# Top-2 dispatch on one core: groups of 64 and 64 rows, eight equal stores, no early store, logits in one transfer

## The chip, the cores and the metric

The kernel runs on one core of a Trainium2 chip. The metric is the device time of one execution in microseconds; lower is better. Before the change the median of three runs is 239.2 us (239.19 to 239.37).

## The reference

For each of 16,384 tokens there are 512 values in `x` and 8 router logits. The two largest softmax probabilities of a token, divided by their sum, become two weights, and the output holds the token's 512 values twice: once times the smaller weight, once times the larger.

```python
probs = np.exp(router_logits - logits_max)
probs = probs / np.sum(probs, axis=-1, keepdims=True)
topk_indices = np.argsort(probs, axis=-1)[..., -k:]          # k = 2
topk_probs = np.take_along_axis(probs, topk_indices, axis=-1)
topk_probs = topk_probs / np.sum(topk_probs, axis=-1, keepdims=True)
x_expanded = x[:, :, np.newaxis, :].repeat(k, axis=2)
return x_expanded * topk_probs[..., np.newaxis]
```

The softmax's denominator cancels, so the two weights are the sigmoid of minus and of plus the difference between the largest and the second largest logit. Read are 33.55 MB of x and 0.52 MB of logits, written are 67.11 MB.

## The kernel before, in words

A *row* below is one token of each of the 128 partitions: 128 x 512 floats, 0.262 MB in x and 0.524 MB in the output, since each value is written twice. There are 128 rows. They are worked off in two groups, `GROUPS = [65, 63]`. Within a group, partition p owns G consecutive tokens (G is 65 or 63), so that one partition's part of a transfer of n rows is one contiguous run of n x 2 KB in x and n x 4 KB in the output. The distance in memory from one partition's run to the next is G x 2 KB in x and G x 4 KB in the output.

Three tiles lie in the core's on-chip memory. `xs` has 65 slots of one x row. `osp` has 18 slots of one output row. `WA` holds the two weights of all 128 rows. The logits are loaded into the last slot of `osp`, and the scratch of the top-2 search lies in the two slots before it.

The work goes in this order, written out by hand in two tables:

- `LOADS` gives the x loads of each group, by their number of rows: 6, 28, 31 for the first group, 32 and 31 for the second. All are issued on the SP queue (line 112). After the first of them come the two logits transfers (lines 105 and 106), and then `top2_weights` (lines 53 to 68): eleven VectorE instructions, which keep the larger and the smaller of pairs of logits, and two sigmoids on ScalarE.
- `STORES` gives for each store the number of rows, the place where the output rows are built (`osp` or `xs`, and the first slot), the number of its rows that ScalarE builds (`by_act`), and the queue. The other rows are built by one VectorE multiplication (line 127). A ScalarE row takes two activations (line 135). Line 138 issues the store.

A store whose home is `xs` is built in place: 16 input rows that sit in the upper half of a region of 32 slots are spread over the whole region as 16 output rows. The stores of a group alternate: one of 16 rows into `osp`, then one in place, then again one into `osp`, which must wait until the earlier store from `osp` has landed, and one of 15 rows in place. The first group has a small store of 2 rows ahead of these, which alone goes through the ACT queue.

Every other transfer is issued by SP, in program order, and SP waits in front of each issue until the data is built or the slots are free. The loads of the second group stand behind the fourth large store of the first group in this order. The second of them writes slots that this store reads, so SP waits until it has landed.

Of the kernel before, what the change touches and what calls it, by code (L numbers as in the profile page):

```python
# [1 line left out]

# [4 lines left out]

F32 = mybir.dt.float32
ALU = mybir.AluOpType
ACTF = mybir.ActivationFunctionType  # L10
P = 128
E = 8
D = 512


GROUPS = [65, 63]
M = sum(GROUPS)


LOADS = [[6, 28, 31], [32, 31]]  # L20


STORES = [
    [
        (2, ("osp", 0), 0, "ACT"),
        (16, ("osp", 2), 0, "SP"),
        (16, ("x", 2), 0, "SP"),
        (16, ("osp", 0), 4, "SP"),
        (15, ("x", 35), 0, "SP"),
    ],  # L30
    [
        (16, ("osp", 0), 1, "SP"),
        (16, ("x", 0), 0, "SP"),
        (16, ("osp", 0), 4, "SP"),
        (15, ("x", 33), 0, "SP"),
    ],
]
OSP = 18


def top2_weights(nc, scratch, logits, WA):

    used = [0]

    def cut(n):
        a = scratch[:, used[0] : used[0] + M * n].rearrange("p (m n) -> p m n", n=n)
        used[0] += M * n
        return a

    a, b = logits[:, :, 0:4], logits[:, :, 4:8]  # L50
    hi = cut(4)
    lo = b
    nc.vector.tensor_tensor(hi, a, b, op=ALU.max)  # L53
    nc.vector.tensor_tensor(lo, a, b, op=ALU.min)  # L54
    n = 4
    while n > 1:
        n //= 2
        a, b = hi[:, :, 0:n], hi[:, :, n : 2 * n]
        nhi, nlo, tmp = cut(n), cut(n), cut(n)
        nc.vector.tensor_tensor(tmp, lo[:, :, 0:n], lo[:, :, n : 2 * n], op=ALU.max)  # L60
        nc.vector.tensor_tensor(nlo, a, b, op=ALU.min)  # L61
        nc.vector.tensor_tensor(nlo, nlo, tmp, op=ALU.max)  # L62
        nc.vector.tensor_tensor(nhi, a, b, op=ALU.max)  # L63
        hi, lo = nhi, nlo
    dlt = cut(1)
    nc.vector.tensor_tensor(dlt, hi, lo, op=ALU.subtract)  # L66
    nc.scalar.activation(WA[:, :, 0], dlt[:, :, 0], ACTF.Sigmoid, scale=-1.0)  # L67
    nc.scalar.activation(WA[:, :, 1], dlt[:, :, 0], ACTF.Sigmoid, scale=1.0)  # L68


@with_exitstack
def kernel(
    ctx: ExitStack,
    tc: tile.TileContext,
    x: bass.AP,
    router_logits: bass.AP,
    k: bass.AP,
    out: bass.AP,
):
    nc = tc.nc  # L80
    N = x.shape[0] * x.shape[1]
    assert int(k) == 2 and router_logits.shape[-1] == E and x.shape[2] == D
    assert N == P * M
    xf = x.rearrange("b s d -> (b s) d")
    of = out.rearrange("b s k d -> (b s) k d")
    rf = router_logits.rearrange("b s e -> (b s) e")
    x_v, o_v, rl_v = [], [], []
    t0 = 0
    for n in GROUPS:
        t1 = t0 + P * n  # L90
        x_v.append(xf[t0:t1].rearrange("(p m) d -> p m d", p=P))
        o_v.append(of[t0:t1].rearrange("(p m) k d -> p m k d", p=P))
        rl_v.append(rf[t0:t1].rearrange("(p m) e -> p m e", p=P))
        t0 = t1

    pool = ctx.enter_context(tc.tile_pool(name="pool", bufs=1))
    xs = pool.tile([P, max(GROUPS), D], F32)
    osp = pool.tile([P, OSP, 2, D], F32)
    WA = pool.tile([P, M, 2], F32)

    logits = osp[:, OSP - 1].rearrange("p k d -> p (k d)").rearrange("p (m e) -> p m e", e=E)
    scratch = osp[:, OSP - 3 : OSP - 1].rearrange("p r k d -> p (r k d)")

    def load_logits():
        nc.sync.dma_start(logits[:, : GROUPS[0]], rl_v[0])  # L105
        nc.sync.dma_start(logits[:, GROUPS[0] :], rl_v[1])  # L106

    m0 = 0
    for g, G in enumerate(GROUPS):
        r = 0  # L110
        for n in LOADS[g]:
            nc.sync.dma_start(xs[:, r : r + n, :], x_v[g][:, r : r + n, :])  # L112
            if g == 0 and r < 6 <= r + n:
                load_logits()
                top2_weights(nc, scratch, logits, WA)
            r += n
        assert r == G
        r = 0
        for n, (home, a), by_act, queue in STORES[g]:
            if home == "x":  # L120
                og = xs[:, a : a + 2 * n, :].rearrange("p (r k) d -> p r k d", k=2)
            else:
                og = osp[:, a : a + n]
            v = n - by_act
            w = WA[:, m0 + r : m0 + r + n, :]
            if v:
                nc.vector.tensor_tensor(  # L127
                    og[:, :v],
                    xs[:, r : r + v, :].unsqueeze(2).to_broadcast([P, v, 2, D]),
                    w[:, :v].unsqueeze(3).to_broadcast([P, v, 2, D]),  # L130
                    op=ALU.mult,
                )
            for i in range(v, n):
                for c in range(2):
                    nc.scalar.activation(  # L135
                        og[:, i, c], xs[:, r + i, :], ACTF.Copy, scale=w[:, i, c : c + 1]
                    )
            {"SP": nc.sync, "ACT": nc.scalar}[queue].dma_start(o_v[g][:, r : r + n], og)  # L138
            r += n
        assert r == G  # L140
        m0 += G


# [1 line left out]
_INS = ['x', 'router_logits', 'k']  # L145
_OUTS = [((16, 1024, 2, 512), 'float32')]

_NUMBERS = {'k': 2}


# [26 lines left out]
```

## Time and profile before

| What | Value |
|---|---|
| median of three runs | 239.2 us |
| the profiled execution, its own time | 239.38 us |
| its span, first to last instruction | 237.6 us |
| VectorE busy | 132.2 us, 20 instructions |
| ScalarE busy | 13.2 us, 21 instructions |
| moved by DMA | 101.19 MB |
| mean rate over the span | 426 GB/s |
| share of the 16 DMA engines' span taken by packets | 97.7% on SP's queue, 1.0% on ACT's |

In the profile DVE is VectorE, ACT is ScalarE, SP is the engine that issues nearly all transfers; SPq and ACTq are their issue queues. q1 is the queue that SP feeds and q10 the one that ACT feeds. Times in a row count from the start of the span. A DMA issue row gives the time from the issue to the moment when the whole transfer has landed.

### The profile page before, as it was taken

The numbers are of one execution on the slowest core, as the hardware profiler recorded it, in microseconds if no ns is written. First come the engines' busy times: TensorE is split into PE (matmuls) and PEld (weight loads), VectorE is DVE, ScalarE is ACT, GpSimd is POOL, SyncE is SP. The second block draws the span as 40 slices with busy tenths as digits, with TensorE's granted clock in tenths as the row PEclk, the third lists the DMA queues.
The fourth block names the chain that finished last, engine by engine and source line by source line (L and its number), as shares of the span: only waits on it lengthen the run. The fifth ranks groups of instructions, "written<-read, shape, count | busy, mean of one in ns | idle before, by whom it ended". The sixth has DMA issues, their size and how long they took to land.

```text
span 237.6 us, 124 instructions
## 1 busy us (share of the span) xinstructions
DVE 132.2 (56%) x20; ACT 13.2 (6%) x21; POOL 0.2 (0%) x4
## 2 busy tenths in 40 slices
DVE  0640599999289999000000009999956999920000
ACT  2000000000080000000000001000006100000000
POOL 0000000000000000000000000000000000000000
DMA  7979989898989989899998989898989989897995
GB/s 265 541 338 488 408 386 535 348 530 353 496 386 441 441 353 530 353 508 414 414 519 353 508 370 502 353 519 353 496 386 419 463 353 530 353 530 342 496 445 217
DMA packets 2304, 101.19 MB, mean 426 GB/s; under 512 B 256, under 2 KB 384, under 8 KB 512
## 3 DMA queue, kind: packets, MB, share of 16 engines
q1 hardware_dynamic: 2160, 100.14, 97.7%
q10 hardware_dynamic: 144, 1.05, 1.0%
HBM read 34.08 MB, written 67.11 MB: 426 GB/s over the span
## 4 chain that ended last, share of the span: by engine, by line
DMA 48%; DVE 39%; SPq 1%; issue 0%; DVEq 0%
DMA xs<-in_x_dram 30%; DVE osp L127 25%; DMA out_dram<-osp 19%; DVE xs L127 14%; SPq L105 0%; SPq L106 0%; SPq L112 0%; SPq L138 0%; DVEq L127 0%
## 5 line engine op out<-in xcount | busy, mean ns | idle before, releaser
L127 DVE TENSOR_TENSOR osp<-xs,WA 128x12288 f32<-128x12288 f32 (+3 forms) x5 | 61.6, 12318 | 68.7 <-DMA xs<-in_x_dram 58.4
L127 DVE TENSOR_TENSOR xs<-xs,WA 128x16384 f32<-128x16384 f32 (+1 forms) x4 | 66.8, 16692 | 0.3
L135 ACT ACTIVATE osp<-xs,WA 128x512 f32<-128x512 f32 x18 | 11.4, 709 | 161.3 <-DMA out_dram<-osp 90.0
L53 DVE TENSOR_TENSOR osp<-osp 128x512 f32<-128x512 f32 x1 | 0.7, 692 | 8.2 <-DMA osp<-in_router_logits_dram 8.2
L67 ACT ACT_TABLE_LOAD x1 | 1.3, 1283 | 0.7 <-PEq L158 0.7
L67 ACT ACTIVATE WA<-osp 128x128 f32<-128x128 f32 x1 | 0.3, 316 | 10.1 <-DVE osp L66 10.1
L54 DVE TENSOR_TENSOR osp<-osp 128x512 f32<-128x512 f32 x1 | 0.7, 693 | 0.0
L60 DVE TENSOR_TENSOR osp<-osp 128x256 f32<-128x256 f32 (+1 forms) x2 | 0.7, 352 | 0.0
L62 DVE TENSOR_TENSOR osp<-osp 128x256 f32<-128x256 f32 (+1 forms) x2 | 0.7, 352 | 0.0
L63 DVE TENSOR_TENSOR osp<-osp 128x256 f32<-128x256 f32 (+1 forms) x2 | 0.7, 352 | 0.0
L61 DVE TENSOR_TENSOR osp<-osp 128x256 f32<-128x256 f32 (+1 forms) x2 | 0.7, 351 | 0.0
L66 DVE TENSOR_TENSOR osp<-osp 128x128 f32<-128x128 f32 x1 | 0.3, 292 | 0.0
L68 ACT ACTIVATE WA<-osp 128x128 f32<-128x128 f32 x1 | 0.3, 298 | 0.0
L158 POOL MEMSET const-bfloat16-1.0<- 128x1 bf16 x1 | 0.1, 102 | 0.0
L158 POOL MEMSET const-uint8-127<- 128x1 uint8 x1 | 0.1, 102 | 0.0
L158 POOL MEMSET const-float32-0.0<- 128x1 f32 x1 | 0.1, 99 | 0.2 <-issue 0.2
L158 POOL MEMSET const-float32-1.0<- 128x1 f32 x1 | 0.1, 99 | 0.0
## 6 DMA issues: line engine op xcount, KB each, us to landing
xs<-in_x_dram SPq DMA_DIRECT2D x2, 7936.0 KB, 40.8
out_dram<-xs SPq DMA_DIRECT2D x2, 7680.0 KB, 27.5
xs<-in_x_dram SPq DMA_DIRECT2D x1, 7168.0 KB, 24.2
xs<-in_x_dram SPq DMA_DIRECT2D x1, 1536.0 KB, 6.0
out_dram<-osp ACTq DMA_DIRECT2D x1, 1024.0 KB, 24.5
osp<-in_router_logits_dram SPq DMA_DIRECT2D x1, 260.0 KB, 6.2
osp<-in_router_logits_dram SPq DMA_DIRECT2D x1, 252.0 KB, 6.4
out_dram<-osp SPq DMA_DIRECT2D x4, 23.9
```

Of the source, the lines that this page charges most:

```text
L53: nc.vector.tensor_tensor(hi, a, b, op=ALU.max)
L54: nc.vector.tensor_tensor(lo, a, b, op=ALU.min)
L60: nc.vector.tensor_tensor(tmp, lo[:, :, 0:n], lo[:, :, n : 2 * n], op=ALU.max)
L61: nc.vector.tensor_tensor(nlo, a, b, op=ALU.min)
L62: nc.vector.tensor_tensor(nlo, nlo, tmp, op=ALU.max)
L63: nc.vector.tensor_tensor(nhi, a, b, op=ALU.max)
L66: nc.vector.tensor_tensor(dlt, hi, lo, op=ALU.subtract)
L67: nc.scalar.activation(WA[:, :, 0], dlt[:, :, 0], ACTF.Sigmoid, scale=-1.0)
L68: nc.scalar.activation(WA[:, :, 1], dlt[:, :, 0], ACTF.Sigmoid, scale=1.0)
L127: nc.vector.tensor_tensor(og[:, :v], xs[:, r : r + v, :].unsqueeze(2).to_broadcast([P, v, 2, D]), w[:, :v].unsqueeze(3).to_broadcast([P, v ...
L135: nc.scalar.activation(og[:, i, c], xs[:, r + i, :], ACTF.Copy, scale=w[:, i, c : c + 1])
L158: nc = _bacc.Bacc("TRN2", target_bir_lowering=False, num_devices=1)
```

## The change

- The groups become 64 and 64 rows. The distance from one partition's run to the next becomes 128 KB in x and 256 KB in the output in both groups.
- The loads of the first group are 6, 28 and 30 rows.
- The early store of 2 rows on the ACT queue goes. The first store of the first group now takes rows 0 to 15, is built in slots 0 to 15 of `osp`, and ScalarE builds two of its rows. All eight stores have 16 rows and are issued by SP.
- Loads and stores name their slots in `xs`. The second group is loaded in 16, 16 and 32 rows: its rows 0 to 15 go first, into slots 16 to 31, then its rows 16 to 31 into slots 0 to 15, then rows 32 to 63 into slots 32 to 63.
- The second group's first store takes rows 16 to 31, that is slots 0 to 15, and builds them in `osp`. Its second store takes rows 0 to 15 from slots 16 to 31 and spreads them in place over slots 0 to 31.
- The logits of both groups come in one transfer.

```diff
-GROUPS = [65, 63]
+GROUPS = [64, 64]
-LOADS = [[6, 28, 31], [32, 31]]
+LOADS = [[(6, 0), (28, 6), (30, 34)], [(16, 16), (16, 0), (32, 32)]]
 STORES = [
     [
-        (2, ("osp", 0), 0, "ACT"),
-        (16, ("osp", 2), 0, "SP"),
-        (16, ("x", 2), 0, "SP"),
-        (16, ("osp", 0), 4, "SP"),
-        (15, ("x", 35), 0, "SP"),
+        (0, 16, 0, ("osp", 0), 2, "SP"),
+        (16, 16, 16, ("x", 0), 0, "SP"),
+        (32, 16, 32, ("osp", 0), 4, "SP"),
+        (48, 16, 48, ("x", 32), 0, "SP"),
     ],
     [
-        (16, ("osp", 0), 1, "SP"),
-        (16, ("x", 0), 0, "SP"),
-        (16, ("osp", 0), 4, "SP"),
-        (15, ("x", 33), 0, "SP"),
+        (16, 16, 0, ("osp", 0), 1, "SP"),
+        (0, 16, 16, ("x", 0), 0, "SP"),
+        (32, 16, 32, ("osp", 0), 4, "SP"),
+        (48, 16, 48, ("x", 32), 0, "SP"),
     ],
 ]
     def load_logits():
-        nc.sync.dma_start(logits[:, : GROUPS[0]], rl_v[0])
-        nc.sync.dma_start(logits[:, GROUPS[0] :], rl_v[1])
+        nc.sync.dma_start(
+            logits.rearrange("p (g m) e -> p g (m e)", g=2),
+            rf.rearrange("(g p m) e -> p g (m e)", g=2, p=P),
+        )
...
-        for n in LOADS[g]:
-            nc.sync.dma_start(xs[:, r : r + n, :], x_v[g][:, r : r + n, :])
+        for n, s in LOADS[g]:
+            nc.sync.dma_start(xs[:, s : s + n, :], x_v[g][:, r : r + n, :])
...
-        for n, (home, a), by_act, queue in STORES[g]:
+        for r, n, s, (home, a), by_act, queue in STORES[g]:
...
-                    xs[:, r : r + v, :].unsqueeze(2).to_broadcast([P, v, 2, D]),
+                    xs[:, s : s + v, :].unsqueeze(2).to_broadcast([P, v, 2, D]),
...
-                        og[:, i, c], xs[:, r + i, :], ACTF.Copy, scale=w[:, i, c : c + 1]
+                        og[:, i, c], xs[:, s + i, :], ACTF.Copy, scale=w[:, i, c : c + 1]
```

A store's entry now reads: first row in the group, number of rows, first input slot, home, rows by ScalarE, queue. A load's entry reads: number of rows, first slot.

More of the change, by code (lines that the diff above doesn't have):

```diff
@@ L117 @@
         assert r == G
-        r = 0
-        for n, (home, a), by_act, queue in STORES[g]:
+        for r, n, s, (home, a), by_act, queue in STORES[g]:
             if home == "x":
@@ L135 @@
                     nc.scalar.activation(
-                        og[:, i, c], xs[:, r + i, :], ACTF.Copy, scale=w[:, i, c : c + 1]
+                        og[:, i, c], xs[:, s + i, :], ACTF.Copy, scale=w[:, i, c : c + 1]
                     )
             {"SP": nc.sync, "ACT": nc.scalar}[queue].dma_start(o_v[g][:, r : r + n], og)
-            r += n
-        assert r == G
         m0 += G
```

## The prediction

> **What bounds the kernel now.** I read the page's slices and queues first, then the chain that ended last, then the transfers one by one.
>
> ```profile
> span 237.6 us, 124 instructions
> ...
> DVE 132.2 (56%) x20; ACT 13.2 (6%) x21; POOL 0.2 (0%) x4
> ...
> GB/s 265 541 338 488 408 386 535 348 530 353 496 386 441 441 353 530 353 508 414 414 519 353 508 370 502 353 519 353 496 386 419 463 353 530 353 530 342 496 445 217
> DMA packets 2304, 101.19 MB, mean 426 GB/s; under 512 B 256, under 2 KB 384, under 8 KB 512
> ...
> q1 hardware_dynamic: 2160, 100.14, 97.7%
> q10 hardware_dynamic: 144, 1.05, 1.0%
> ```
>
> The queues' packets fill 98.7% of the span, VectorE 56%. The slices swing between 338 and 541 GB/s, yet none between first and last falls away. The chain of waits nevertheless names VectorE for 39% of the span, so the question is whether the DMA engines ever stood still for it. The issues on SP's queue, in order of time, answer that together with each issue's time to landing:
>
> ```profile
> 2.10 1.11 SPq L112 DMA_DIRECT2D xs<-in_x_dram  x2
> 43.61 0.35 SPq L138 DMA_DIRECT2D out_dram<-osp  x1
> 60.87 0.34 SPq L138 DMA_DIRECT2D out_dram<-xs  x1
> 78.98 0.33 SPq L138 DMA_DIRECT2D out_dram<-osp  x1
> 95.20 0.33 SPq L138 DMA_DIRECT2D out_dram<-xs  x1
> 95.58 27.65 SPq L112 DMA_DIRECT2D xs<-in_x_dram  x2
> 158.32 0.34 SPq L138 DMA_DIRECT2D out_dram<-osp  x1
> 175.60 0.34 SPq L138 DMA_DIRECT2D out_dram<-xs  x1
> 193.24 0.33 SPq L138 DMA_DIRECT2D out_dram<-osp  x1
> 209.45 0.33 SPq L138 DMA_DIRECT2D out_dram<-xs  x1
> ```
>
> The DMA issue view, asked for one stretch at a time (the last column is us from issue to landing; in order of issue: the 31-row load of group 1, its second, third and fourth large store, the 31-row load of group 2, its first, second and fourth store; the third again shows 25.5):
>
> ```profile
> xs<-in_x_dram SPq DMA_DIRECT2D x1, 7936.0 KB, 43.8
> ...
> out_dram<-xs SPq DMA_DIRECT2D x1, 24.3
> ...
> out_dram<-osp SPq DMA_DIRECT2D x1, 25.5
> ...
> out_dram<-xs SPq DMA_DIRECT2D x1, 7680.0 KB, 27.7
> ...
> xs<-in_x_dram SPq DMA_DIRECT2D x1, 7936.0 KB, 37.9
> ...
> out_dram<-osp SPq DMA_DIRECT2D x1, 21.8
> ...
> out_dram<-xs SPq DMA_DIRECT2D x1, 23.8
> ...
> out_dram<-xs SPq DMA_DIRECT2D x1, 7680.0 KB, 27.3
> ```
>
> And pieces of the chain, in order of time:
>
> ```profile
> 2.10 24.16 DMA xs<-in_x_dram
> ...
> 26.35 17.24 DVE osp L127
> ...
> 43.61 22.22 DMA out_dram<-osp
> ...
> 95.58 46.42 DMA xs<-in_x_dram
> ...
> 142.10 16.17 DVE osp L127
> ```
>
> Issue plus time to landing gives the landings. The 28-row load: 2.10 + 24.16 = 26.26. The 31-row load: its issue is the second half of the 2.10 row, about 2.68, so 46.5. The stores of group 1: 65.8, 85.2, 104.5, 122.9. The loads of group 2: 142.0, and 160.8 (issued in the last 0.34 us of the 27.65 us row, about 122.9). Its stores: 180.1, 199.4, 218.7, 236.75. The steps between them are 19.3 us for every store of 16 rows (8.39 MB, 434 GB/s), 18.0 to 18.4 for 15 rows, 19.1 for 32 x rows, 18.8 for 31. From 46.5 to 236.75 are 190.3 us for 82.58 MB: 2.304 us per MB, without a step that sticks out. So the transfers run end to end, and VectorE sits on the chain only because its waits are as long as the transfers. What decides the time is the 101.19 MB at this price (233.1 us), what is lost ahead (the 18.61 MB up to 46.5 would need 42.9, so their effective start is at 3.6), and 0.85 us from the last landing to the span's end.
>
> **How early a store must be issued.** Two stores are issued with little queued before them. The first of group 1 at 43.61, 2.9 us before the landing of the load ahead (46.5); the first of group 2 at 158.32, 2.5 us before 160.8. Both land 19.3 us behind that load, as stores issued five us ahead do. So 2.5 us of lead cost nothing; smaller leads the trace does not show.
>
> **The change part by part.** Durations of the building instructions, by form:
>
> ```profile
> L127 DVE TENSOR_TENSOR osp<-xs,WA 128x12288 f32<-128x12288 f32 x2 | 25.9, 12958 | 9.8 <-DMA out_dram<-osp 9.8
> L127 DVE TENSOR_TENSOR osp<-xs,WA 128x16384 f32<-128x16384 f32 x1 | 17.2, 17226 | 11.4 <-DMA xs<-in_x_dram 11.4
> L127 DVE TENSOR_TENSOR osp<-xs,WA 128x15360 f32<-128x15360 f32 x1 | 16.2, 16157 | 46.9 <-DMA xs<-in_x_dram 46.9
> L135 ACT ACTIVATE osp<-xs,WA 128x512 f32<-128x512 f32 x18 | 11.4, 709 | 161.3 <-DMA out_dram<-osp 90.0 <-DMA xs<-in_x_dram 71.2
> ```
>
> *Bytes.* Reads and writes stay 101.19 MB, so at 2.304 us per MB this term is unchanged: the two rows of the early store come back in the two stores that grow from 15 to 16 rows, and the row that group 1 loses group 2 loads.
>
> *Early store.* It goes with its 2.29 us multiplication, at 12.63, when VectorE next waits 11.43 us for a load, so both were free. Its 1.05 MB (2.4 us) now leave with a later store. They had shared the engines with the loads:
>
> ```profile
> 14.95 0.37 ACTq L138 DMA_DIRECT2D out_dram<-osp  x1
> ```
>
> ```profile
> out_dram<-osp ACTq DMA_DIRECT2D x1, 1024.0 KB, 24.5
> ```
>
> It landed at 39.45, so some of it ran ahead of the 28-row load. Without it this load ends when its own 9.44 MB (6 + 28 rows and logits) are through: 3.6 + 21.7 = 25.3 instead of 26.26. The 30-row load then lands at 46.5 less 1.31 MB (one x row and the early store, 3.0 us), 43.5.
>
> *First store.* Here the cover is thinnest, since the early store had stretched the time under which VectorE builds. VectorE has 14 rows: 12.96 + 2 x 1.07 (a row, from 12 rows at 12.96 and 16 at 17.23) = 15.1. It starts at 25.4 and ends at 40.5. ScalarE's two rows are 4 x 0.709 = 2.8 us beside it. Issue at 40.5, a lead of 2.9 us on 43.5: nothing lost. Had VectorE all 16 rows, the lead would be 0.8.
>
> *The other stores of group 1.* Each step is 19.33 us. Second store: issue 57.8, the one ahead lands at 62.8. Third: waits for that landing, plus 12.96, issue 75.9 against 82.1. Fourth: 93.1 against 101.5. Leads of 5.0, 6.2 and 8.3 us; nothing lost.
>
> *Second group's loads.* The split adds one issue (0.3 to 0.4 us of SP, at 93, when it has 27 us to spare). Both 16-row loads write slots 0 to 31, free since the second store landed at 82.1. The 32-row load waits for the fourth store's landing, as the 31-row load did, at 120.8; behind it in SP's queue stands only a store that is built after 156. Landings 130.4, 140.1 and 159.4. The first store takes the half that lands second, so it starts at 140.1 and not at 130.4: the split alone starts nothing earlier. Issue at 140.2 + 16.16 = 156.4, a lead of 3.0. The later stores have 5.1, 6.2 and 8.3, and the last lands at 159.4 + 77.3 = 236.7.
>
> *Logits in one transfer.* The first load and the two logits transfers:
>
> ```profile
> xs<-in_x_dram SPq DMA_DIRECT2D x1, 1536.0 KB, 6.0
> ...
> osp<-in_router_logits_dram SPq DMA_DIRECT2D x1, 260.0 KB, 6.2
> osp<-in_router_logits_dram SPq DMA_DIRECT2D x1, 252.0 KB, 6.4
> ```
>
> Issued at about 0.73, 1.16 and 1.64 (each issue takes about 0.4 us, and the 2.10 row follows), they landed at 6.7, 7.4 and 8.0. The first load's 1.57 MB need 3.6 us, so its effective start is 3.1. Between it and the 3.6 above lie 0.5 us, lost to the logits and to the early store's mixing with the loads. That is the most that can be gained. On the other side, one transfer lands its second half no faster than two did: 0. The second logits transfer took 0.7 us for 0.26 MB, 0.6 at full rate: 0.1 for one transfer fewer; as much again for the early store's small pieces. I take 0.2. The weights are needed at 25.4 and may come late at no cost.
>
> **Sum.** The last landing is at 236.75 - 0.2 = 236.55, the span 237.4. Against the profiled execution's own 239.38 that makes 239.2. The median of the runs lies 0.18 below that execution, so I forecast 239.0.
>
> **Row pitch, weighed.** With 64 rows the runs of neighbouring partitions lie exactly 128 KB (x) and 256 KB (output) apart; before they were 130 and 260, 126 and 252 KB. The trace has no power of two to show: 260 and 252 KB give the same 19.3 us per store. By the Trainium skill, "DMA: Bandwidth & Descriptors", section "Latency and other measured facts", copies whose rows lie 512 KiB apart ran at 207 GB/s and padded ones at 214, with much worse at 2 MiB and above. That is a rule against this change; its smallest pitch is twice ours. Were its 3.4% true at 256 KB, the eight stores would take 5.2 us more by that page's estimate, about 244. The same page's section "Bandwidth" has 16 MB loads to 128 partitions, which is 128 KiB each, at 425 GB/s, and so speaks for the loads being safe.
>
> **The rivals.**
> 1. *Slower: the equal pitch slows the stores.* The eight stores hold 8 x 19.33 = 154.6 us of the path, with no slack anywhere. It decides from 0.09 us per store (0.45%), which puts the time above 239.7. How far steady rates differ in this trace bounds it:
>
> ```profile
> 85.00:104.00 19.00, 10.17 (x1) 0.00 (x0) 0.00 (x0) 1.00 0.99 428
> ...
> 160.30:179.60 19.30, 15.27 (x1) 0.00 (x0) 0.00 (x0) 1.00 1.00 435
> ```
>
> Between nothing and 1.6% (428 against 435 GB/s), the middle is 0.8%, 1.2 us: 240.2; at the end 241.5. For it: an untried address pattern on the resource that is full. Against it: 126 to 260 KB show no trend. Chance 0.16.
> 2. *Slower: the first store comes too late.* If the 28-row load lands at 26.26 as before, the lead is 2.0, below anything shown. A hole would be about the missing 0.5 to 1 us: 239.7 to 240.0. Chance 0.06.
> 3. *Faster: the start's loss goes with the small transfers.* If the whole 0.5 us goes instead of 0.2: 238.7, on the edge; with a tenth from elsewhere 238.6. Against it: the logits' 256 pieces stay, as does the first load's latency. Chance 0.08.
> 4. *The split helps nothing*, which is already in the sum: its store waits for the second half.
>
> **How the numbers follow.** Forecast 0.70. The three runs lie 0.08% apart; 0.2% is 0.48 us, about what a measurement of this kernel can tell from no change. Within it lies 238.7 to 239.7, hence same 0.70, slower 0.16 + 0.06 = 0.22, faster 0.08. The range takes in the third rival's edge, the second and the first's middle: 238.5 to 240.6; the forecast's own is 238.7 to 239.5.
>
> **What would show it.** Right: landings of stores still 19.3 us apart, 43.3 for the 30-row load, store issues near 40.5 and 156.4, the last landing at 236.5. A step of 19.5 or more for every store shows rival 1; one long step behind the first store rival 2; an effective start at or below 3.1 rival 3. If a wait appears that the slots do not need, for instance a 16-row load issued only when the fourth store has landed, the second group's start would slip and the prediction be wrong.

## The result and the profile after

The changed kernel takes 239.92 us (median of 8 runs, 239.5 to 240.19) against 239.28 us for the kernel before (8 runs, 239.18 to 239.37): a ratio of 1.0023, 95% interval 1.0015 to 1.0032. It is slower, by 0.6 us. The forecast's own value, 239.0 us, was 0.9 us too low and on the wrong side of the kernel before. The time lies above the forecast's own 238.7 to 239.5 and inside the wide range only through the room that was left there for the rivals. The runs of the changed kernel also scatter over 0.7 us, those of the kernel before over 0.2.

The page of the changed kernel, span and transfers:

```profile
span 238.0 us, 127 instructions
...
DVE 129.9 (55%) x19; ACT 15.7 (7%) x25; POOL 0.2 (0%) x4
...
DMA packets 2288, 101.19 MB, mean 425 GB/s; under 512 B 240, under 2 KB 240, under 8 KB 496
...
q1 hardware_dynamic: 2288, 101.19, 98.7%
```

Bytes and fill are as before: 98.7% of 16 engines' span. A busy share cannot show this loss, since a packet (one partition's run in one transfer, carried by one DMA engine) that takes longer counts as busy. The landings show it. SP's issues in the changed kernel, in order of time:

```profile
1.64 0.99 SPq L115 DMA_DIRECT2D xs<-in_x_dram  x2
40.38 0.35 SPq L140 DMA_DIRECT2D out_dram<-osp  x1
57.65 0.34 SPq L140 DMA_DIRECT2D out_dram<-xs  x1
75.69 0.33 SPq L140 DMA_DIRECT2D out_dram<-osp  x1
92.97 0.33 SPq L140 DMA_DIRECT2D out_dram<-xs  x1
93.36 28.09 SPq L115 DMA_DIRECT2D xs<-in_x_dram  x3
156.75 0.34 SPq L140 DMA_DIRECT2D out_dram<-osp  x1
...
209.59 0.33 SPq L140 DMA_DIRECT2D out_dram<-xs  x1
```

The DMA issue view of the changed kernel, one stretch at a time (last column: us from issue to landing), in order of issue: the 30-row load, the four stores of group 1, the loads of 16, 16 and 32 rows, the first and the last store of group 2:

```profile
xs<-in_x_dram SPq DMA_DIRECT2D x1, 7680.0 KB, 41.1
...
out_dram<-osp SPq DMA_DIRECT2D x1, 22.2
...
out_dram<-xs SPq DMA_DIRECT2D x1, 24.2
...
out_dram<-osp SPq DMA_DIRECT2D x1, 25.5
...
out_dram<-xs SPq DMA_DIRECT2D x1, 28.1
...
xs<-in_x_dram SPq DMA_DIRECT2D x1, 4096.0 KB, 37.5
...
xs<-in_x_dram SPq DMA_DIRECT2D x1, 4096.0 KB, 45.9
...
xs<-in_x_dram SPq DMA_DIRECT2D x1, 38.7
...
out_dram<-osp SPq DMA_DIRECT2D x1, 22.4
...
out_dram<-xs SPq DMA_DIRECT2D x1, 27.5
```

Issue plus time to landing, with the issues of the second and the third load of the 93.36 row at 94.63 and 121.1 (three issues in one row; the last one ends the row and takes 0.33). The forecast's column has the 0.2 us of the start taken off:

| Transfer | before: landed | step | after: landed | step | forecast |
|---|---|---|---|---|---|
| last load of group 1 | 46.5 | | 43.2 | | 43.3 |
| first store | 65.8 | 19.3 | 62.6 | 19.3 | 62.6 |
| second store | 85.2 | 19.4 | 81.8 | 19.3 | 81.9 |
| third store | 104.5 | 19.3 | 101.2 | 19.4 | 101.3 |
| fourth store | 122.9 | 18.4 (15 rows) | 121.1 | **19.9** | 120.6 |
| loads of group 2 | 142.0, 160.8 | 19.1, 18.8 | 130.9, 140.5, 159.8 | **9.8**, 9.7, 19.3 | 159.2 |
| last store | 236.75 | | 237.1 | | 236.55 |

Up to the third store everything lies within 0.1 us of the forecast. The 0.55 us that are missing at the end arise at one place: the fourth store takes 19.9 instead of 19.33 us, and the first load behind it another 0.1. After that the steps are 19.3 again. That is the point at which the DMA engines change from writing group 1's output to reading group 2's x, called the hand-over below. The records of single packets narrow it down further: the last 16 packets of the fourth store, one per engine, took 2.56 to 3.04 us in the changed kernel, while the 64 KB packets ahead of them took 2.42. In the kernel before, the last 16 (60 KB) took 2.27 to 2.38 and those ahead 2.27.

To compare kernels whose stores differ in rows, I use one number from the landings, the **hand-over excess**: the time from the landing of the transfer ahead of group 1's last store to the landing of group 2's last load, less its bytes at 2.304 us per MB. For the kernel before it is 160.79 - 104.48 = 56.31 us against 56.17 for 24.38 MB: 0.14 us. For the changed kernel it is 159.82 - 101.19 = 58.63 against 57.98 for 25.17 MB: 0.65 us. It is good to about 0.1 us, as the times to landing are given in tenths. The **lead** of the first large store is the landing of the load ahead less the store's issue: 46.48 - 43.61 = 2.87 us before, 43.24 - 40.38 = 2.86 us after.

### The profile page after: what moved, and what is told of

It reads as the page before. It is cut to its first block, busy times and chain, and to the rows that moved or that the text cites. A ratio compares the mean times of both kernels' runs of the same rounds, so it can differ in the third digit from the quotient of the medians.

```text
span 238.0 us, 127 instructions
## 1 busy us (share of the span) xinstructions
DVE 129.9 (55%) x19; ACT 15.7 (7%) x25; POOL 0.2 (0%) x4
## 2 busy tenths in 40 slices
DMA packets 2288, 101.19 MB, mean 425 GB/s; under 512 B 240, under 2 KB 240, under 8 KB 496
## 3 DMA queue, kind: packets, MB, share of 16 engines
q1 hardware_dynamic: 2288, 101.19, 98.7%
## 4 chain that ended last, share of the span: by engine, by line
DMA 48%; DVE 39%; SPq 1%; issue 0%; DVEq 0%
DMA xs<-in_x_dram 29%; DVE osp L129 24%; DMA out_dram<-osp 19%; DVE xs L129 14%; SPq L115 1%; SPq L106 0%; SPq L140 0%; DVEq L129 0%
## 5 line engine op out<-in xcount | busy, mean ns | idle before, releaser
L129 DVE TENSOR_TENSOR osp<-xs,WA 128x12288 f32<-128x12288 f32 (+2 forms) x4 | 57.2, 14292 | 71.1 <-DMA xs<-in_x_dram 60.7
L129 DVE TENSOR_TENSOR xs<-xs,WA 128x16384 f32<-128x16384 f32 x4 | 68.9, 17226 | 0.4
L137 ACT ACTIVATE osp<-xs,WA 128x512 f32<-128x512 f32 x22 | 13.9, 710 | 157.8 <-DMA xs<-in_x_dram 85.5
```

What stands on the lines that cost most here:

```text
L129: nc.vector.tensor_tensor(og[:, :v], xs[:, s : s + v, :].unsqueeze(2).to_broadcast([P, v, 2, D]), w[:, :v].unsqueeze(3).to_broadcast([P, v ...
L137: nc.scalar.activation(og[:, i, c], xs[:, s + i, :], ACTF.Copy, scale=w[:, i, c : c + 1])
```

## The experiments

The table has all kernels. Each median is of 4 to 11 executions, and each ratio is to the kernel before on the same chip, whose median lay between 239.20 and 239.28 us in all these comparisons. *Pitch* is the distance in memory from one partition's run to the next; "equal" means groups of 64 and 64 rows. Lead and excess come from the one profiled execution of each kernel, which can lie apart from the median: f1's took 240.53 us, k2's 240.00, m1's 239.54 and e3's 239.43.

| Kernel | pitch | lead, us | excess, us | median, us (range) | ratio, 95% interval |
|---|---|---|---|---|---|
| before | 65/63 | 2.9 | 0.1 | 239.28 (239.18 to 239.37) | |
| changed | equal | 2.9 | 0.65 | 239.92 (239.5 to 240.19) | 1.0015 to 1.0032 |
| changed, loaded again | equal | 2.9 | 1.25 | 240.15 (239.31 to 240.27) | 1.0019 to 1.0043 |
| e1 changed, one load | equal | 2.8 | 0.75 | 239.85 (239.43 to 240.51) | 1.0014 to 1.0032 |
| e2 before, split | 65/63 | 2.9 | 0.2 | 239.31 (239.16 to 239.46) | 0.9992 to 1.0009 |
| e3 before, equal pitch | equal | 2.3 | 0.35 | 239.56 (239.33 to 240.27) | 1.0007 to 1.0024 |
| m1 e3, lead taken back | equal | 2.8 | 0.3 | 239.82 (239.35 to 240.09) | 1.0013 to 1.0034 |
| f1 changed, early store back | equal | 2.3 | 1.3 | 239.90 (239.67 to 240.53) | 1.0021 to 1.0046 |
| f4 changed, loads held back | equal | 2.8 | 0.65 | 239.78 (239.4 to 240.45) | 1.0016 to 1.0033 |
| f5 changed, twice the pitch | 2 x equal | 3.3 | 1.35 | 240.94 (240.75 to 241.17) | 1.0058 to 1.0085 |
| h2 changed, groups exchanged | equal | 2.8 | 0.35 | 239.46 (239.22 to 240.22) | 1.0000 to 1.0022 |
| k2 changed, earlier first store | equal | 3.6 | 0.7 | 240.46 (239.84 to 240.53) | 1.0031 to 1.0056 |
| k1 before, later first store | 65/63 | 2.2 | 0.4 | 239.48 (239.4 to 241.08) | 1.0005 to 1.0030 |
| e4 65/63, no early store, 17-row store | 65/63 | 3.9 | 0.55 | 239.92 (239.81 to 240.0) | 1.0016 to 1.0035 |
| f2 e4, later first store | 65/63 | 2.4 | 2.1 | 241.18 (240.67 to 241.32) | 1.0066 to 1.0091 |
| g1 f2, loaded again | 65/63 | 2.4 | 2.3 | 241.46 (241.11 to 241.77) | 1.0080 to 1.0106 |
| h1 f2, groups exchanged | 65/63 | 2.4 | 1.65 | 241.04 (240.65 to 241.19) | 1.0063 to 1.0089 |
| g3 65/63, no early store, 1-row store | 65/63 | 4.1 | 0.2 | 239.75 (239.64 to 240.13) | 1.0016 to 1.0033 |
| k3 g3, first store between | 65/63 | 3.4 | 0.25 | 239.52 (239.34 to 240.05) | 1.0003 to 1.0021 |
| h3 g3, later first store | 65/63 | 2.3 | 1.9 | 241.14 (240.24 to 241.49) | 1.0062 to 1.0091 |

### First set: which part of the change costs it

Theories: A, the two 16-row loads queued behind the fourth store; B, the equal power-of-two pitch; C, the missing early store or the single logits transfer.

**e1**, the split undone in the changed kernel:

```diff
-LOADS = [[(6, 0), (28, 6), (30, 34)], [(16, 16), (16, 0), (32, 32)]]
+LOADS = [[(6, 0), (28, 6), (30, 34)], [(32, 0), (32, 32)]]
-        (16, 16, 0, ("osp", 0), 1, "SP"),
-        (0, 16, 16, ("x", 0), 0, "SP"),
+        (0, 16, 0, ("osp", 0), 1, "SP"),
+        (16, 16, 16, ("x", 0), 0, "SP"),
```

> The changed kernel, but the second group's first 32 rows come in one load of 32 rows (its first store takes slots 0 to 15, as before the change). Theory A (the loss sits where group 1's fourth store hands over to two 16-row loads queued behind it): back to 239.2 us or a little less, no packet trouble at about 118 us. Theory B (equal power-of-two row pitch): stays at 239.9. Theory C (removing the early store or the single logits transfer costs it): stays at 239.9.

Measured 239.85 us, the excess still 0.75.

**e2**, the split alone in the kernel before:

```diff
-LOADS = [[6, 28, 31], [32, 31]]
+LOADS = [[(6, 0), (28, 6), (31, 34)], [(16, 16), (16, 0), (31, 32)]]
-        (16, ("osp", 0), 1, "SP"),
-        (16, ("x", 0), 0, "SP"),
+        (16, 16, 0, ("osp", 0), 1, "SP"),
+        (0, 16, 16, ("x", 0), 0, "SP"),
```

> The kernel before, with the second group's first load split into 16 and 16 rows in the changed kernel's slots and order, nothing else. Theory A: 239.9 us, the loss behind the fourth store. Theories B and C: 239.3 us, like the kernel before.

Measured 239.31 us. Theory A falls from both sides: the split does nothing to the time, as the forecast had it.

**e3**, groups of 64 alone in the kernel before:

```diff
-GROUPS = [65, 63]
+GROUPS = [64, 64]
-LOADS = [[6, 28, 31], [32, 31]]
+LOADS = [[6, 28, 30], [32, 32]]
-        (15, ("x", 35), 0, "SP"),
+        (14, ("x", 36), 0, "SP"),
...
-        (15, ("x", 33), 0, "SP"),
+        (16, ("x", 32), 0, "SP"),
```

> The kernel before with groups of 64 and 64 rows (stores of 2, 16, 16, 16, 14 and four times 16 rows, loads 6, 28, 30 and 32, 32), two logits transfers, early store kept. Theory B: 239.9 us. Theories A and C: 239.3 us.

Measured 239.56 us, slower by 0.3, with runs up to 240.27: about half of what the changed kernel loses. That fits part of B. But the shorter last load also shortened the first store's lead to 2.3 us (m1 comes back to that), and the rows of several transfers change together with the pitch: the last load of group 1 has 30 rows, its last store 14, the last load and the last store of group 2 have 32 and 16.

**e4**, the changed kernel with the old pitch:

```diff
-GROUPS = [64, 64]
+GROUPS = [65, 63]
-LOADS = [[(6, 0), (28, 6), (30, 34)], [(16, 16), (16, 0), (32, 32)]]
+LOADS = [[(6, 0), (28, 6), (31, 34)], [(16, 16), (16, 0), (31, 32)]]
-        (32, 16, 32, ("osp", 0), 4, "SP"),
-        (48, 16, 48, ("x", 32), 0, "SP"),
+        (32, 17, 32, ("osp", 0), 4, "SP"),
+        (49, 16, 49, ("x", 33), 0, "SP"),
...
-        (48, 16, 48, ("x", 32), 0, "SP"),
+        (48, 15, 48, ("x", 33), 0, "SP"),
```

> The changed kernel with groups of 65 and 63 rows (stores of 16, 16, 17, 16 and 16, 16, 16, 15 rows, two logits transfers since the groups differ), no early store, split loads. Theory A: 239.9 us. Theory B: 239.2 us. Theory C: 239.9 us.

Measured 239.92 us, and narrow (239.81 to 240.0). So the equal pitch is not the only thing that can cost this much. Part of it sits elsewhere: the load ahead of the first store landed at 44.2 us, 0.5 later than in f2 below.

### Second set: early store, depth of the queue, size of the pitch

**f1**, the early store put back into the changed kernel:

```diff
-        (0, 16, 0, ("osp", 0), 2, "SP"),
-        (16, 16, 16, ("x", 0), 0, "SP"),
-        (32, 16, 32, ("osp", 0), 4, "SP"),
-        (48, 16, 48, ("x", 32), 0, "SP"),
+        (0, 2, 0, ("osp", 0), 0, "ACT"),
+        (2, 16, 2, ("osp", 2), 0, "SP"),
+        (18, 16, 18, ("x", 2), 0, "SP"),
+        (34, 16, 34, ("osp", 0), 4, "SP"),
+        (50, 14, 50, ("x", 36), 0, "SP"),
```

> The changed kernel with the early store of 2 rows put back on the ACT queue (group 1 stored in 2, 16, 16, 16, 14 rows; the rest as changed). So far groups of 64 cost 0.3 us with the early store and 0.6 us without. Theory D (dropping the early store costs 0.3 to 0.6 us by itself): about 239.55, as with groups of 64 alone. Theory E (only the equal pitch costs, and its size is chance): 239.5 to 239.9, no different from the changed kernel.

Measured 239.90 us: no better than without it. So at groups of 64 the missing early store is not what costs. The run shows something else as well. It differs from e3 (239.56) only in the split, which did nothing in e1 and e2, and in the single logits transfer, the other half of theory C.

**f2**, e4 with a later first store:

```diff
-        (0, 16, 0, ("osp", 0), 2, "SP"),
+        (0, 16, 0, ("osp", 0), 1, "SP"),
```

> The 65/63 kernel without the early store, with one row of the first store on ScalarE instead of two, so that this store is issued 1.07 us later (about 41.4), 1.0 to 1.4 us before the load ahead has sent its last bytes. Theory F (a store issued before the engines begin their last packets of the load ahead costs 0.4 us at that place; all leads without loss so far lay under 1.9 us): the 0.4 us behind the last load of group 1 goes, about 239.5. Theory G (the hand-over cost hangs on addresses or on the missing early store): stays at 239.9.

Both theories missed. (The leads of this expectation count to the last bytes sent and not, as in the table, to the landing.) The load ahead did land earlier, at 43.7 instead of 44.2, and the kernel still became 1.3 us slower: the excess at the hand-over, 80 us later, rose to 2.1.

**f4**, the loads of the changed kernel held back:

```diff
     for g, G in enumerate(GROUPS):
+        if g == 1:
+            nc.vector.tensor_tensor(
+                xs[:, 0:32, :], xs[:, 0:32, :], xs[:, 0:32, :], op=ALU.max
+            )
         for n, s in LOADS[g]:
```

> The changed kernel with one extra VectorE instruction of 17.2 us on slots 0 to 31 behind the fourth store's build, so that group 2's two 16-row loads are issued at about 110 instead of 93 us, when only the fourth store is in the queue. The instruction's values are overwritten by the loads. Theory H (a load queued 25 us deep behind two stores is what makes the hand-over slow; its issue took 1.2 us instead of 0.33): loss at 118 us gone, about 239.2. Theory B (equal pitch at the change from writing to reading): stays at 239.9.

The loads were issued at 110.15 instead of 93.36; 239.78 us, excess 0.65 as before. Theory H falls.

**f5**, twice the pitch: each partition owns 128 consecutive tokens.

```diff
-        x_v.append(xf[t0:t1].rearrange("(p m) d -> p m d", p=P))
-        o_v.append(of[t0:t1].rearrange("(p m) k d -> p m k d", p=P))
+        x_v.append(xp[:, t0 : t0 + n])      # xp = xf.rearrange("(p m) d -> p m d", p=P)
+        o_v.append(op[:, t0 : t0 + n])      # op = of.rearrange("(p m) k d -> p m k d", p=P)
...
+        nc.sync.dma_start(logits, rf.rearrange("(p m) e -> p m e", p=P))
```

> The changed kernel with each partition owning 128 consecutive tokens over both groups, so that the runs lie 256 KB (x) and 512 KB (output) apart instead of 128 and 256 KB; logits in one run of 4 KB per partition. Theory B in the form that steady stores suffer: stores of 19.5 us and more, above 241. Theory B at the hand-over alone: stores stay at 19.3, the loss at 118 us as large or larger, 239.9 to 240.5. If pitch plays no part: 239.9, unchanged in its place as well.

Measured 240.94 us. SP's issues of this kernel from the third store to the loads:

```profile
76.13 0.33 SPq L135 DMA_DIRECT2D out_dram<-osp  x1
93.42 0.33 SPq L135 DMA_DIRECT2D out_dram<-xs  x1
93.80 28.48 SPq L110 DMA_DIRECT2D xs<-in_x_dram  x3
```

and its issues to landing (third store, fourth store, 32-row load):

```profile
out_dram<-osp SPq DMA_DIRECT2D x1, 25.6
...
out_dram<-xs SPq DMA_DIRECT2D x1, 28.5
...
xs<-in_x_dram SPq DMA_DIRECT2D x1, 39.1
```

The third store lands at 101.7, the fourth at 121.9 (20.2 us), the last load at 121.95 + 39.1 = 161.05: excess 1.35. The second and the third store still land 19.4 us behind the one ahead. So twice the pitch leaves steady stores as they are and makes the hand-over worse. The time lies above the 240.5 of theory B at the hand-over alone, and the hand-over is not all of it: the last load of group 1 landed at 43.66, 0.4 later than in the changed kernel. The transfers have the same rows here, and the first store is issued at 40.36 instead of 40.38; besides the pitch, the groups' places in memory and the layout of the logits change.

### Third set: does it belong to the program, and is there a version without it

**g1** is f2 again (on another chip) and **g2** the changed kernel again, each in a fresh load.

> The 65/63 kernel with the later first store, unchanged, in a fresh load on the chip. It came out at 241.2 us, 1.3 us over its twin with one row more on ScalarE, and even its undisturbed stores were 19.36 instead of 19.32 us apart. Theory K (the loss belongs to the program): 241.2 again. Theory L (it belongs to where a load of the program puts its tensors in memory, or to the chip): some other time, 239.3 to 240.

> The changed kernel, unchanged, in a fresh load. Theory K: 239.9 again, with runs spread over half a us. Theory L: a median that differs from 239.9 by more than 0.2 us.

g1 gave 241.46 us after 241.18, so f2's loss goes with its program and not with a chip or a load. g2 gave 240.15 after 239.92. That is 0.23 apart, just over the 0.2 of theory L, but its runs (239.31 to 240.27) spread over 1 us and cover all of the first load's, so g2 does not decide between the two. The size of the loss varies from execution to execution. The profiled execution of g2 took 240.27 us of its own, 0.5 more than the changed kernel's first profile (239.76), and shows where the scatter sits. SP's issues of g2:

```profile
75.55 0.33 SPq L140 DMA_DIRECT2D out_dram<-osp  x1
92.83 0.33 SPq L140 DMA_DIRECT2D out_dram<-xs  x1
93.21 28.00 SPq L115 DMA_DIRECT2D xs<-in_x_dram  x3
```

and its issues to landing (third store, fourth store, the 32-row load issued at 120.9):

```profile
out_dram<-osp SPq DMA_DIRECT2D x1, 25.5
...
out_dram<-xs SPq DMA_DIRECT2D x1, 28.0
...
xs<-in_x_dram SPq DMA_DIRECT2D x1, 39.4
```

101.05 for the third store, 160.3 for the last load: 59.25 us against 58.0, excess 1.25. The excess is 0.6 us larger than in the first profile, the execution 0.5 us longer.

**g3**, the old pitch without early store, without split, with the odd row by itself (against e4):

```diff
-LOADS = [[(6, 0), (28, 6), (31, 34)], [(16, 16), (16, 0), (31, 32)]]
+LOADS = [[(6, 0), (28, 6), (31, 34)], [(32, 0), (31, 32)]]
-        (32, 17, 32, ("osp", 0), 4, "SP"),
+        (32, 16, 32, ("osp", 0), 4, "SP"),
+        (48, 1, 48, ("osp", 16), 0, "SP"),
```

> Groups of 65 and 63 rows, no early store, first store with two rows on ScalarE, no split, and no transfer with more than 64 KB per partition: the odd row of group 1 is stored by itself behind the third store. Theory M (only equal pitch, or rows over 64 KB, make the hand-overs slow): 239.0, the kernel before less the 0.3 us that the start gains without the early store. Theory D (dropping the early store costs it by itself): 239.6 to 239.9.

Measured 239.75 us, a time that theory D had forecast, too. The hand-over is clean (0.2), as M had it, but the load ahead of the first store landed late, and that ate the gain.

### Fourth set: addresses or moments

**h1** and **h2** exchange the two groups' places in memory, in f2 and in the changed kernel (h2 also has two logits transfers):

```diff
-    t0 = 0
+    t0 = N
     for n in GROUPS:
-        t1 = t0 + P * n
+        t1, t0 = t0, t0 - P * n
...
-        t0 = t1
```

> The 65/63 kernel with the later first store (241.2 and 241.5 us), with the two groups' places in memory exchanged: the group worked first takes the last 65 x 128 tokens. Instructions and sizes are the same, only addresses differ. Theory N (the hand-over's loss and the slightly slow stores come from which addresses are read and written together): a time that differs by 0.5 us or more, 239.3 to 240.5. Theory F (they come from the moment of the issues): 241.2 to 241.5 again.

> The changed kernel with the two groups' places in memory exchanged and the logits in two transfers. Theory N with equal pitch as the cause: still 239.7 to 240.2 with the loss behind the fourth store, since both groups keep the same pitch. If the particular addresses of this hand-over matter and not the pitch: 239.0 to 239.4 or above 240.4.

h1: 241.04 us, so the 241 us kernels do not hang on these addresses. h2: 239.46 us, between the two answers; its runs still reach 240.22.

**h3** is g3 with a later first store (the same line as f2).

> The 65/63 kernel without early store and without the split, its odd row stored by itself (239.75 us, 0.6 us of it lost behind the last load of group 1), with one row of the first store on ScalarE instead of two, so that this store is issued 1.07 us later. Theory F (a store that stands in the queue before the engines begin the last packets of the load ahead slows these): the 0.6 us goes, nothing is lost behind the fourth store, 239.1, below the kernel before. Theory N: 239.7, or some other time above 239.4.

Measured 241.14 us where F had 239.1. g3's first-store issue and its 31-row load:

```profile
40.20 0.35 SPq L137 DMA_DIRECT2D out_dram<-osp  x1
```

```profile
xs<-in_x_dram SPq DMA_DIRECT2D x1, 7936.0 KB, 41.7
```

h3's, and its 32-row load behind the fourth store:

```profile
41.28 0.35 SPq L137 DMA_DIRECT2D out_dram<-osp  x1
```

```profile
xs<-in_x_dram SPq DMA_DIRECT2D x1, 7936.0 KB, 40.9
...
xs<-in_x_dram SPq DMA_DIRECT2D x1, 49.8
```

Issued at 2.62 and 2.71, the loads land at 44.3 (g3) and 43.6 (h3): a store issued 1.1 us earlier makes the load ahead of it land 0.7 us later. In h3 the load behind the fourth store, issued at 93.90, lands only at 143.7.

**k1** tries the moment by itself: the kernel before plus one short VectorE instruction ahead of the first large store's.

```diff
+            if g == 0 and n == 16 and r < 16:
+                z = xs[:, 32:34].rearrange("p r d -> p (r d)")[:, :512]
+                nc.vector.tensor_tensor(
+                    osp[:, OSP - 1].rearrange("p k d -> p (k d)")[:, :512], z, z, op=ALU.max
+                )
```

> The kernel before with one extra VectorE instruction of about 0.65 us (one row's maximum with itself into a slot of osp that the first large store overwrites), placed so that it delays the first large store's issue from 43.6 to about 44.25; nothing else. Theory Q (the moment of the first large store's issue, measured from the start of the engines' last packets of the load ahead, decides how slow the later change from stores to loads is: 0.57 us in the kernel before with no loss there, 1.1 to 1.2 us in the 241 us kernels): loss of 0.3 us or more behind the fourth store, 239.6 to 241. Theory P (equal pitch or the missing early store decides): 239.3, unchanged.

SP's issues in k1:

```profile
44.07 0.35 SPq L142 DMA_DIRECT2D out_dram<-osp  x1
...
78.78 0.33 SPq L142 DMA_DIRECT2D out_dram<-osp  x1
...
95.38 27.70 SPq L112 DMA_DIRECT2D xs<-in_x_dram  x2
```

and to landing (third large store; 32-row load, 31-row load of group 2):

```profile
out_dram<-osp SPq DMA_DIRECT2D x1, 25.5
...
xs<-in_x_dram SPq DMA_DIRECT2D x1, 46.7
...
xs<-in_x_dram SPq DMA_DIRECT2D x1, 7936.0 KB, 38.1
```

Third store at 104.3, last load (issued at 122.74) at 160.8: excess 0.4, and 239.48 us, 0.23 over the kernel before. One of its 11 runs took 241.08, the others 239.4 to 239.8. No hole opens behind the first store; the loss appears 75 us later. The size is below what theory Q wanted (239.6 to 241). So at the old pitch a shift of one issue by 0.46 us alone makes an excess like that of e3 and m1. (In the packets' records the last packets of the load ahead begin 0.2 us before this issue in the kernel before and 0.8 in k1. The expectation's 0.57 and 1.1 to 1.2 put their start about 0.3 us earlier; the differences between the kernels are about the same.)

**k2** issues the changed kernel's first store earlier: three rows on ScalarE, and k1's instruction with 640 elements.

> The changed kernel with three instead of two rows of the first store on ScalarE and an extra VectorE instruction of about 0.8 us ahead of its 13 rows, so that this store is issued about 0.25 us earlier, at 40.1 instead of 40.4. Theory Q: the moment becomes that of the kernel before or a little earlier, the loss behind the fourth store shrinks to under 0.1 us, about 239.0 to 239.3 (or 0.1 to 0.4 us more if some of the load's last packets suffer). Theory P with equal pitch: loss stays at 0.3 to 0.4 us there, 239.7 to 240.1.

Issued at 39.85; 240.46 us, excess 0.7. Theory Q fails for the changed kernel, and the time lies above theory P's 240.1 as well.

**k3** is g3 with k1's instruction of 384 elements.

> The 65/63 kernel without early store and without the split (first store issued at 40.2: 239.75 us, with 0.6 us lost behind the load ahead; issued at 41.3: 241.14 us, with 0.8 and 0.55 us lost behind the fourth store), with an extra VectorE instruction of about 0.5 us ahead of the first store's 14 rows, so that it is issued at about 40.7. Theory Q: neither loss, 239.0 to 239.1, below both neighbours and below the kernel before. Theory D (the missing early store costs by itself): between its neighbours, 239.8 to 241.

239.52 us: below both neighbours, as Q alone had it, but 0.5 us above Q's value and not below the kernel before. Its last load of group 1 still landed at 44.0, 0.3 later than h3's.

**m1** keeps e3's equal pitch and takes the lead back to 2.8 us: one row of the first large store on ScalarE, and k1's instruction.

> Groups of 64 and 64 rows in the kernel before (239.56 us), but with the first large store issued at the moment that the kernel before has: one of its rows on ScalarE (1.07 us earlier) and an extra VectorE instruction of about 0.6 us ahead of its 15 rows, so that it is issued about 0.5 us earlier, 0.57 us behind the start of the engines' last packets of the load ahead instead of 1.05. Theory Q (the moment alone): no loss behind the fourth store, 239.25. Theory B (equal pitch by itself): loss of 0.25 us and more there, 239.5 to 239.7, as without the shift.

239.82 us, no better than e3's 239.56 and above both theories. Groups of 64 cost time with the lead of the kernel before, too.

## Why the prediction was wrong

**Right.** The bytes and their price: steady stores stay 19.3 us apart. The start: the last load of group 1 landed at 43.24 where the kernel before, less one row and the early store (3.02 us), would have been at 43.46: 0.2 us gained, as forecast. That the sum was met is partly luck, since half of it was put down to the logits: h2, with two logits transfers, lands this load at 43.24 as well, so no gain of the single transfer shows. The first store, the thinnest cover, lost nothing: issue 40.38, forecast 40.5. The second group's first store was issued at 156.75 against 156.4, late by what its loads were late. The split does nothing (e1, e2). Removing the early store is not what costs at groups of 64 (f1).

**The step that failed** is in "Second group's loads": landings 130.4, 140.1 and 159.4 with nothing lost. I took the price of 2.304 us per MB for every transfer with enough queued behind it, and looked for loss only where a queue could run dry. This queue was full, 25 us deep, and the loss came all the same, where the engines change from stores to loads: 0.65 us in one profile, 1.25 in the other. In the kernel before the same change costs 0.1, and the forecast carried that over to the changed kernel without a term of its own. Over the runs it is 0.1 to 2.3 us. The place of the loss is shown; which part of the change causes it is shown only in part.

**Rival 1** named a suspect that the runs bear out in part, with the wrong mechanism. Equal pitch slows no steady store (19.3 us at 256 KB, 19.4 at 512 KB between output runs), so what it costs isn't paid "from 0.09 us per store" but at one hand-over. That its 240.2 us lies near 239.92 and 240.15 is luck. Its bound, 428 against 435 GB/s, was misread: the first of these windows has 19.0 us and does not fit its store. By their landings both stores take 19.3 us.

For the equal pitch speak e3 (0.3 us), m1 (0.6 us, lead kept) and f5, where twice the pitch adds 1 us. They don't isolate it: in e3 and m1 the rows of some transfers change with it, in f5 the places in memory. All nine programs with equal or twice equal pitch have medians over that of the kernel before (h2's interval reaches down to no change), but seven of the eight other programs with 65 and 63 rows are slower than it as well.

**A rival that no run tries alone** is the single logits transfer. Among these nine programs the three with two logits transfers (e3, m1, h2) have excesses of 0.3 to 0.35 us, and the six with one (changed, e1, f1, f4, f5, k2) have 0.65 or more. The medians lean the same way, but overlap (239.46 to 239.82 against 239.78 and more), and the profiled executions of e3, m1 and h2 were among the faster of theirs. From f1 against e3, about half of the loss may come from that part of the change; that is not shown. The changed kernel with two logits transfers and nothing else altered would tell.

The rule that was weighed under "Row pitch", from the Trainium skill, "DMA: Bandwidth & Descriptors", section "Latency and other measured facts", has 3% at a pitch of 512 KiB for copies within HBM. The traces do not agree for stores from on-chip memory: f5 has that pitch in its output, and its second and third stores keep 19.4 us.

**Account of the profiled executions.** Own times 239.76 and 239.38, 0.38 apart; last landings 237.10 and 236.80 in the traces (the 236.75 above comes from a time to landing given in tenths), 0.30 apart. The start gains 0.22 and the hand-over loses 0.65 - 0.14 = 0.51, which makes 0.29. The median lies 0.16 higher than this execution; the second profile indicates that such differences sit at the hand-over as well.

**Open.** Why equal pitch would slow this change from writing to reading is not settled; that reads and writes of many engines fall on the same part of the memory is a guess that no run here separates. h2, which exchanged addresses at equal pitch, was 0.5 to 0.7 us faster than the changed kernel, with two logits transfers besides; which of the two did it wasn't tried, and the intervals of the ratios overlap. Nor is it settled why the first store's moment acts 75 us later at the old pitch: 0.2 us in k1, 1.4 us in h3 against g3. No version that I ran beats the kernel before.

## What to carry to other kernels

A DMA-bound kernel whose queue never runs dry can still lose time where its transfers change direction. Read landings, not busy shares: put the landings in order, take each step less its bytes at the steady price, and see at which transfer the difference arises. When all covers hold and a change still moves the row pitch, the sizes of transfers or one issue by half a microsecond, give the change of direction a price of its own: at the one from stores to loads it was 0.1 to 2.3 us here. And when a change has several parts, undo each of them alone.

## What the runs showed of the hardware that I had not expected

- A store issued earlier can make the load ahead of it land later: 44.3 us with the store issued at 40.20 (g3), 44.0 at 40.60 (k3), 43.6 at 41.28 (h3). The last 16 packets of this load took 2.59 to 3.23 us in g3, 2.34 to 2.80 in k3 and 2.34 to 2.35 in h3; in g3 they began at 40.39, behind the issue, in h3 at 40.37, ahead of it.
- The moment of a single issue has no monotone effect: with the first store at 40.20, 40.60 and 41.28 (g3, k3, h3, otherwise the same work) the time was 239.75, 239.52 and 241.14 us. Two losses pull against each other: the early issue goes with the late load above, the late one with the excess of 1.9 us at the hand-over.
- Issuing a load took SP 1.2 us instead of 0.33 behind two queued transfers: in the changed kernel the issue at 93.36 is followed by the next only at 94.63. In f4, with one store ahead, the first of these loads took 0.34 and the second, behind store and load, 1.26. The kernel before has the same long issue (1.14 at 95.58) and next to no loss at the hand-over, so this alone is not its cause.
